# Quarter sums on DVE, LayerNorm's scale and shift on transposed tiles (ACT) and later on h (GpSimd), in a hybrid decoder layer on one core

## Chip, cores and metric

The kernel runs on 1 core of one Trainium2 chip. The metric is the device time of one launch in microseconds (us). The version before takes 1103.41 us, the median of three runs between 1101.94 and 1104.91. Engines are named as the profile names them: PE is the matrix engine (TensorE), DVE is VectorE, ACT is ScalarE, POOL is GpSimd, and SP is the engine that issues all the DMAs here.

## The reference

One decoder layer over 512 rows of 1024 numbers, in float32, in four steps that each end with a LayerNorm over `ALPHA*x + step(x)`:

```python
h = LN1(ALPHA*h + 0.5*swiglu(h, w_ffn1_in, w_ffn1_out))     # silu(gate)*up, 1024 -> 2816 -> 1024
h = LN2(ALPHA*h + mixer(h))     # HGRN2 heads (chunks of 64) and causal pooling, then w_mix_out
h = LN3(ALPHA*h + cross_attention(h, mem))                  # 4 heads, 256 memory tokens
h = LN4(ALPHA*h + 0.5*swiglu(h, w_ffn2_in, w_ffn2_out))
# LN(x, g, b) = (x - mean) * rsqrt(var + eps) * g + b, over the 1024 numbers of a row
```

## The kernel before

**Number format.** A float32 operand is split into two parts of a reduced matmul format: ACT casts the source (`hi`, line 65), DVE subtracts the cast from the source (`lo`, line 66), and PE sums three products, hi·hi, hi·lo and lo·hi (lines 54 to 56 in projections, 248 to 250 in `out_gemm`, 366 in the feed-forward). So each block of weights and each activation costs a cast, a subtraction and, for a weight, a DMA of 512 KB from SP.

**Feed-forward (`ffn`).** The 2816 hidden columns go in 22 blocks of 128 (the first two of ffn1 by plain products, "first"). Each other block multiplies a gate and an up weight as quarters, by seven products instead of eight: `a11`, `a12`, `s1`, `s4`, `s2`, `s3`, `a22`, each of 12 matmuls of 128x256 with a weight "quad" (128x512, a cast and a subtraction). Four sums per block, done on POOL (`sums`, lines 345 to 348), make the quarters s1 to s4 of the weight, in the buffers into which it was loaded. On the side of the activations the quarters `b11`, `b21`, `b22` are parts of the transposed input, and `t1` to `t4` are sums of them: for ffn1 sums of x on POOL (line 122), for ffn2 made while the third LayerNorm's tiles are transposed (`transpose_quarters`). Blocks go in pairs; one group of two blocks (two groups in ffn2) has its `a12` and `a11` started ahead. A pair is 168 matmuls.

**Output product and LayerNorm (`out_gemm`).** Each of the four steps ends here: two halves of 512 columns, and in each four accumulators for the four tiles t of 128 rows. In the second half the last four blocks of weights are kept, so that the tiles end one after the other, tile 0 first. At a tile's end DVE adds `alpha*h` (line 263), takes the statistics (266, 172, 174), POOL raises the variance to the power -1/2 (`rstd`, 176), and DVE applies everything in `ln_tile`: `(h - mean)*G`, then `*rstd + B`, each as two halves (lines 178 to 184), with G and B as rows broadcast to all partitions. Then PE transposes the tile by eight 128x128 matmuls against `ident` (line 191, into `trh`), and the transposed parts are split straight from PSUM into the tiles of the next step's input (`f1T` for the mixer, `moT` for attention, `xob`/`xot` for ffn2). The last step writes to the output instead.

**Mixer.** It projects with `wf`, `wq`, `wg`, `wi` and `wv`, then makes the scores within a chunk by levels m = 1 to 64 (`lv1` to `lv64`, line 553). Each level multiplies, in two halves, by QP and KR; behind each half DVE multiplies that half of QP and KR in place by decays (`Tlev`, lines 567 and 568) for the next level. POOL makes the decays (546) and, at four levels, the pooling windows (`pl`, 504 to 509).

**What sets the order.** A framework schedules the instructions at build time and writes one fixed list for each engine; on the chip each list is executed strictly in order, and an instruction that waits holds all behind it. Buffers come from pools: `raw` (7 of 128x1024, where every weight lands, and G and B too), `q` (7 split weights), `b8` (13 large ones), `sm` (small ones). A DMA into a buffer can start only when the last reader of what was there is done, and SP issues its DMAs in order too.

Of the kernel before, what the change touches and what calls it, by code (L numbers as in the profile page):

```python
# [23 lines left out]
H = 4  # L24
# [9 lines left out]
def layer_kernel(ctx: ExitStack, tc: tile.TileContext, a, out):  # L34
# [82 lines left out]
    xs = [b8([P, 2, 4, 256], F32, f"xs{i}") for i in range(2)]  # L117
    for n, t, x, y in (("t1", xs[0][:, 0], xf[0][:, :, lo_], xf[0][:, :, hi_]),
                       ("t2", xs[0][:, 1], xs[0][:, 0], xf[1][:, :, hi_]),
                       ("t3", xs[1][:, 0], xf[0][:, :, hi_], xf[1][:, :, hi_]),  # L120
                       ("t4", xs[1][:, 1], xs[0][:, 1], xf[1][:, :, lo_])):
        nc.gpsimd.tensor_tensor(out=t, in0=x, in1=y, op=ALU.add)
        T = quarter(f"x{n}")
        split(t, T[:, :, 0, :], T[:, :, 1, :])
        xq[n] = parts(T)
# [3 lines left out]
    masks = const.tile([P, len(LEVELS), 64], F32, name="masks")  # L129
    nc.sync.dma_start(masks, a["masks"])  # L130
    masks = masks.bitcast(I32)
    identu = ident.bitcast(I32)
    recip = const.tile([P, 16], F32, name="recip")
    nc.sync.dma_start(recip, a["recip"].partition_broadcast(P))
    mhalf = const.tile([P, 4], F32, name="mhalf")
    nc.vector.memset(mhalf, -0.5)
    hlb = const.tile([P, 2, H], F32, name="hlb")
    nc.sync.dma_start(hlb, a["hgrn_lb"])
    gn = const.tile([P, 1], F32, name="gn")
    nc.sync.dma_start(gn, a["gnorm"])  # L140
# [12 lines left out]
    nc.vector.tensor_tensor(out=lsum, in0=le[:, 0, :], in1=le[:, 1, :], op=ALU.add)
    nc.vector.reciprocal(lsum, lsum)
    lb = const.tile([P, H], F32, name="lb")
    nc.vector.tensor_tensor(out=lb, in0=le[:, 0, :], in1=lsum, op=ALU.mult)
    oml = const.tile([P, H], F32, name="oml")
    nc.vector.tensor_scalar(oml, lb, -1.0, 1.0, op0=ALU.mult, op1=ALU.add)

# [3 lines left out]
    def ln_bcast(g, b):  # L163
        G, B = raw4([P, D], "G"), raw4([P, D], "B")
        nc.sync.dma_start(G, g.partition_broadcast(P))
        nc.sync.dma_start(B, b.partition_broadcast(P))
        return G, B

    def ln_tile(t, stats, GB, eps):
        G, B = GB  # L170
# [5 lines left out]
        nc.gpsimd.tensor_tensor(out=rstd, in0=ve, in1=mhalf[:, 0:1], op=ALU.pow)  # L176
        for hf in range(2):
# [4 lines left out]
            nc.vector.scalar_tensor_tensor(  # L182
                out=h[t][:, sl], in0=h[t][:, sl], scalar=rstd, in1=B[:, sl],
                op0=ALU.mult, op1=ALU.add)

    def transpose_h(t, tiles):
        for hf in range(2):
            ps = tr_ps(f"trh{t}{hf}")
            for j in range(4):
                k = hf * 4 + j  # L190
                nc.tensor.transpose(ps[:, j * P:(j + 1) * P], h[t][:, k * P:(k + 1) * P], ident)
            pv = ps.rearrange("p (a b n) -> p a b n", a=2, b=2)
            for q in range(2):
                T = tiles[hf * 2 + q]
                tsl = slice(t * P, (t + 1) * P)
                split(pv[:, q], T[:, :, 0, tsl], T[:, :, 1, tsl])

    def transpose_quarters(t, q, f):
# [3 lines left out]
        pv = []  # L202
        for hf in range(2):
            ps = tr_ps(f"trh{t}{hf}")
            for j in range(4):
                k = hf * 4 + j
                nc.tensor.transpose(ps[:, j * P:(j + 1) * P], h[t][:, k * P:(k + 1) * P], ident)
            pv.append(ps.rearrange("p (k n) -> p k n", k=4))
# [3 lines left out]

        if t < 2:
            for hf in range(2):
                into(f"b{hf + 1}1", pv[hf])
                nc.scalar.copy(out=f["lo"][:, hf, :, usl], in_=pv[hf])
            return
        acc, low, b12 = f["lo"][:, 0, :, usl], f["lo"][:, 1, :, usl], f["b12"][:, :, usl]
        nc.vector.tensor_tensor(out=acc, in0=acc, in1=pv[0], op=ALU.add)
        into("t1", acc)  # L220
        nc.scalar.copy(out=b12, in_=pv[0])
        into("b22", pv[1])
        nc.vector.tensor_tensor(out=acc, in0=acc, in1=pv[1], op=ALU.add)
        into("t2", acc)
        nc.vector.tensor_tensor(out=b12, in0=b12, in1=pv[1], op=ALU.add)
        into("t3", b12)
        nc.vector.tensor_tensor(out=acc, in0=acc, in1=low, op=ALU.add)
# [601 lines left out]
```

## Time and profile before

| | |
|---|---|
| median of three runs | 1103.41 us (1101.94 to 1104.91) |
| the profiled execution, its own time | 1105.94 us |
| its span | 1104.1 us |
| PE busy | 1071.0 us, 97% (6782 instructions) |
| DVE busy | 779.4 us, 71% |
| ACT busy | 457.7 us, 41% |
| POOL busy | 324.0 us, 29% |
| transfers on SP's queue | 112.78 MB, mean 102 GB/s of HBM reads and writes over the span |

Read it so. The span is the time between the first and the last instruction of one profiled execution, some 2 us less than that execution's own time. An engine's busy time is the sum of its instructions; on PE a matmul counts as busy from its modelled start to its end. In the lists below, a row such as `a<-b 128x512 x4 | ...` names the tile that is written, those that are read, its shape and how often it comes. A part in brackets, `[4.39 <-PE f1ps L250]`, is the idle time ahead of the instruction on its engine, and what ended it. In the timeline the first number is the start in us from the span's beginning, the second the duration. In the windows view the first pair is the stretch.

The stages lie as follows: start of ffn1 14 to 46 us, its loop to about 242, its output product to about 360, mixer to 560, attention to 750, ffn2 from 750 on.

### The profile page before, as it was taken

Reading aid. Unit: us, or ns where it says so; the run is one execution under the profiler, and the core shown is the slowest. Engines: PE = TensorE matmul, PEld = TensorE weight load, DVE = VectorE, ACT = ScalarE, POOL = GpSimd, SP = SyncE. Lnnn points to the kernel's source line nnn. Section 1 sums busy time; section 2 is a strip of 40 time slices with the busy share of each in tenths; the row PEclk is TensorE's granted clock in tenths of the full one; section 3 lists DMA queues with packets and bytes.
Section 4 is the critical chain, followed back from the end, with each engine's and each line's share of the span. In section 5 each row is a group of like instructions: output and inputs, shape, how many; then the busy total and the mean of one; then the engine's idle time right before and its main releaser. Section 6 shows DMA issues by size and latency. Waiting matters only on the chain.

```text
span 1104.1 us, 17228 instructions
## 1 busy us (share of the span) xinstructions
PE 1071.0 (97%) x6782; PEld 970.4 (88%) x6782; DVE 779.4 (71%) x1160; ACT 457.7 (41%) x812; POOL 324.0 (29%) x226
## 2 busy tenths in 40 slices
PE   8799999999999999999999999977999999999997
PEld 7799999998888888889888988856999999988885
DVE  7899999984425633675786356488999999982416
ACT  6455555572211332224324345044555555572210
POOL 5666756700000020401010000017567576400001
PEclk9999999999999999999999999988999999999999
DMA  7324233263331322212427411111332432443402
GB/s 278 144 87 143 77 114 116 78 181 100 112 127 44 115 77 77 86 58 80 138 68 220 125 58 56 59 39 58 113 118 77 126 104 80 149 135 96 134 1 76
DMA packets 34495, 113.87 MB, mean 103 GB/s; under 512 B 4336, under 2 KB 5616, under 8 KB 34416
## 3 DMA queue, kind: packets, MB, share of 16 engines
q1 hardware_dynamic: 34416, 112.78, 31.9%
q8 instruction: 53, 0.87, 0.3%
q14 instruction: 26, 0.21, 0.1%
HBM read 110.67 MB, written 2.10 MB: 102 GB/s over the span
## 4 chain that ended last, share of the span: by engine, by line
PE 91%; DVE 3%; DMA 2%; POOL 1%; issue 1%; ACT 1%; SPq 0%; DVEq 0%; ACTq 0%; POOLq 0%
PE f2u L366 11%; PE f1u L366 10%; PE f2v L366 5%; PE f1v L366 5%; PE f1ps L248 4%; PE f1ps L249 4%; PE f1ps L250 4%; PE f2ps L250 4%; PE f2ps L248 4%; PE f2ps L249 4%; PE f2w L366 3%; PE f1w L366 2%; PE lv L553 2%; PE pxq L56 1%; PE pxq L54 1%; PE pxq L55 1%
## 5 line engine op out<-in xcount | busy, mean ns | idle before, releaser
L176 POOL TENSOR_TENSOR rstd<-ve,mhalf 128x1 f32<-128x1 f32 x16 | 15.5, 970 | 482.3 <-DVE ve L174 482.3
L66 DVE TENSOR_TENSOR wlo_f<-raw_f,whi_f 128x1024 fp32r<-128x1024 f32 x40 | 48.8, 1223 | 98.5 <-PE f1ps L249 46.4
L65 ACT CAST whi_f<-raw_f 128x1024 fp32r<-128x1024 f32 x40 | 42.1, 1052 | 113.4 <-PE f2ps L250 55.3
L366 PE MATMUL f2u<-xot,qf2s 128*128 128x256 f32 x528 | 68.4, 287 | 3.1 <-DVE f2sg L380 3.1
L366 PEld LDWEIGHTS f2u<-xot,qf2s 128*128 128x128 f32 x528 | 66.1, 195 | 3.6 <-DVE f2sg L380 3.6
L248 PE MATMUL f1ps<-whi_f,f1gs 128*128 128x512 f32 x160 | 62.5, 390 | 0.0
L249 PE MATMUL f1ps<-wlo_f,f1gs 128*128 128x512 f32 x160 | 62.3, 389 | 0.0
L249 PE MATMUL f2ps<-wlo_f,f2gs 128*128 128x512 f32 x160 | 62.3, 389 | 0.0
L248 PE MATMUL f2ps<-whi_f,f2gs 128*128 128x512 f32 x160 | 62.3, 389 | 0.0
L250 PE MATMUL f1ps<-whi_f,f1gs 128*128 128x512 f32 x160 | 62.1, 391 | 0.0
L250 PE MATMUL f2ps<-whi_f,f2gs 128*128 128x512 f32 x160 | 61.9, 390 | 0.0
L366 PE MATMUL f1u<-xt,qf1s 128*128 128x256 f32 x480 | 60.7, 283 | 0.0
L366 PEld LDWEIGHTS f1u<-xt,qf1s 128*128 128x128 f32 x480 | 59.0, 192 | 0.0
L66 DVE TENSOR_TENSOR qf2a<-raw_f2g,qf2a 128x512 fp32r<-128x512 f32 x44 | 53.2, 1214 | 7.9 <-ACT qf2a L65 6.7
L345 POOL TENSOR_TENSOR f2s<-raw_f2u 128x512 f32<-128x512 f32 x22 | 35.5, 1615 | 72.7 <-DMA raw_f2u<-in_w2in 69.9
L66 DVE TENSOR_TENSOR qf1a<-raw_f1g,qf1a 128x512 fp32r<-128x512 f32 x40 | 50.3, 1261 | 7.2 <-ACT qf1a L65 6.4
L366 PE MATMUL f2u<-xob,qf2a 128*128 128x256 f32 x264 | 39.0, 296 | 9.6 <-ACT qf2a L65 6.1
L345 POOL TENSOR_TENSOR f1s<-raw_f1u 128x512 f32<-128x512 f32 x20 | 31.2, 1561 | 57.9 <-DMA raw_f1u<-in_w1in 37.8
L366 PEld LDWEIGHTS f2u<-xob,qf2a 128*128 128x128 f32 x264 | 35.7, 203 | 11.2 <-ACT qf2a L65 7.0
L366 PE MATMUL f2w<-xob,qf2a 128*128 128x256 f32 x264 | 36.7, 290 | 2.0 <-DVE qf2a L66 0.8
L347 POOL TENSOR_TENSOR raw_f2g<-f2s,raw_f2g 128x512 f32<-128x512 f32 x22 | 36.7, 1669 | 0.9 <-DVE qf2a L66 0.6
L366 PEld LDWEIGHTS f2w<-xob,qf2a 128*128 128x128 f32 x264 | 34.1, 197 | 2.7 <-DVE qf2a L66 1.0
(325 smaller groups left out, 3135.8 us busy)
## 6 DMA issues: line engine op xcount, KB each, us to landing
raw_f<-in_w1out SPq DMA_DIRECT2D x22, 512.0 KB, 3.8
raw_f2g<-in_w2in SPq DMA_DIRECT2D x22, 512.0 KB, 3.7
raw_f2u<-in_w2in SPq DMA_DIRECT2D x22, 512.0 KB, 4.5
raw_f<-in_w2out SPq DMA_DIRECT2D x22, 512.0 KB, 3.7
raw_f1g<-in_w1in SPq DMA_DIRECT2D x20, 512.0 KB, 4.3
raw_f1u<-in_w1in SPq DMA_DIRECT2D x20, 512.0 KB, 4.5
raw_wk<-in_wk SPq DMA_DIRECT2D x8, 512.0 KB, 3.9
raw_mo<-in_wmixo SPq DMA_DIRECT2D x8, 512.0 KB, 3.6
```

What stands on the lines that cost most here:

```text
L54: nc.tensor.matmul(o, lh, rh, start=first, stop=False)
L55: nc.tensor.matmul(o, lh, rl, start=False, stop=False)
L65: nc.scalar.copy(out=hi, in_=src)
L66: nc.vector.tensor_tensor(out=lo, in0=src, in1=hi.bitcast(F32), op=ALU.subtract)
L176: nc.gpsimd.tensor_tensor(out=rstd, in0=ve, in1=mhalf[:, 0:1], op=ALU.pow)
L248: nc.tensor.matmul(ps[t], ah[:, tsl], wh, start=i == 0 and j == 0, stop=False)
L249: nc.tensor.matmul(ps[t], ah[:, tsl], wl, start=False, stop=False)
L250: nc.tensor.matmul(ps[t], al[:, tsl], wh, start=False, stop=i == nb - 1 and j == 1)
L345: nc.gpsimd.tensor_tensor(out=s1, in0=a21, in1=a22, op=ALU.subtract)
L347: nc.gpsimd.tensor_tensor(out=a11, in0=s1, in1=a11, op=ALU.subtract)
L366: nc.tensor.matmul(o, q[:, w, wsl], x[k][r], start=opens and k == 0 and n == 0, stop=ends and k == 3 and n == 2, skip_group_check=True)
L553: nc.tensor.matmul(ps[:, i * 64:(i + 1) * 64].rearrange("p (n m) -> p n m", m=m), KR[:, hd, cs], rhs, start=True, stop=True)
```

## The change

Nothing of what is computed changes, apart from rounding.

1. **Weight sums of the feed-forward** (`sums`) go from POOL to DVE.
2. **Sums of x** for ffn1 (`x_sums`) go from POOL to DVE, and stand behind the first two blocks' `a12` and `a11` instead of ahead of everything.
3. **LayerNorm 1 to 3.** `normalize` no longer applies G and B. DVE makes `nmr = -mean*rstd`, ACT applies `rstd*h + nmr` in two halves of 128x512, PE transposes, and ACT applies the scale and shift of each column while it moves the transposed parts to SBUF: after the transpose a column is a partition, so these are eight Identity activations of 128x128 a tile with one number per partition from a new constant `lnT`. The result `y` is then split.
4. **h itself** gets its scale and shift later (`restore`): eight operations of 128x1024 on POOL for each of the three LayerNorms, programmed at the head of the next `out_gemm`, with G and B loaded there. The final LayerNorm (`ln_final`) is as before.
5. **Quarters for ffn2** are added from the SBUF tiles y on DVE; t4 comes only after the last tile.
6. **Order of the blocks.** A block's `a12` and `a11` are begun by a rule (`begin(4)`: at most four blocks open) after s4 and s2 and after s3 of a pair; ffn1 opens with 2 blocks, ffn2 with 3 instead of 4. One more split weight block is kept in `b8` (`head + 3`).
7. **Constants of the mixer** (masks, recip, hlb and what is worked out from it) stand behind ffn1 in the program.

```diff
-        nc.gpsimd.tensor_tensor(out=t, in0=x, in1=y, op=ALU.add)
+    def x_sums():
+            nc.vector.tensor_tensor(out=t, in0=x, in1=y, op=ALU.add)
...
-    def ln_tile(t, stats, GB, eps):
+    def normalize(t, stats, eps):
+        mv, rstd = moments(stats, eps)
+        nc.vector.tensor_scalar(nmr, mv[:, 0:1], rstd, -1.0, op0=ALU.mult, op1=ALU.mult)
+        for hf in range(2):
+            sl = slice(hf * 512, hf * 512 + 512)
+            nc.scalar.activation(h[t][:, sl], h[t][:, sl], AF.Identity, scale=rstd, bias=nmr)
+    def restore(ln, g, b):
+        G, B = rows(g, "G"), rows(b, "B")
+        for t in range(NT):
+            nc.gpsimd.tensor_tensor(out=h[t], in0=h[t], in1=G, op=ALU.mult)
+            nc.gpsimd.tensor_tensor(out=h[t], in0=h[t], in1=B, op=ALU.add)
...
+    def transposed(t, hf, y, ln):
+            nc.tensor.transpose(ps[:, j * P:(j + 1) * P], h[t][:, k * P:(k + 1) * P], ident)
+            nc.scalar.activation(y[:, j, :], ps[:, j * P:(j + 1) * P], AF.Identity,
+                                 scale=lnT[:, ln, 0, k:k + 1], bias=lnT[:, ln, 1, k:k + 1])
...
-            ws = [wblock(wsrc[hf, order[i]], f"{name}{hf}_{i}", stay=hf == 1 and i < head + 2) for i in range(head, nb)]
-            if hf == 1:
-                GB = ln_bcast(g, b)
+            ws = [wblock(wsrc[hf, order[i]], f"{name}{hf}_{i}", stay=hf == 1 and i < head + 3) for i in range(head, nb)]
+            if hf == 1 and final:
+                GB = rows(g, "G"), rows(b, "B")
...
-            nc.gpsimd.tensor_tensor(out=s1, in0=a21, in1=a22, op=ALU.subtract)
+            nc.vector.tensor_tensor(out=s1, in0=a21, in1=a22, op=ALU.subtract)
...
+            begin(4)
+            for j in two:
+                product(j, "s3")
+            begin(4)
```

The change moves instructions; three places show it.

PE at the end of ffn1's output product, before. `f1ps` are the accumulators, `h_306` and `h_307` the tiles t = 2 and 3 of h, `trh` the transposes, and `pf` the mixer's first two projections, which read the transposed input `f1T` and the weights wf0 and wf1 (`whi_wf`, `wlo_wf`):

```order
L250 MATMUL f1ps_3290<-whi_f_10_3495,f1gs_3210 128x512
L191 MATMUL trh_3660<-ident,h_306 128x128 x4
L248 MATMUL f1ps_3290<-whi_f_10_3495,f1gs_3210 128x512
L249 MATMUL f1ps_3290<-wlo_f_10_3496,f1gs_3210 128x512
L250 MATMUL f1ps_3290<-whi_f_10_3495,f1gs_3210 128x512
L54 MATMUL pf_3739<-f1T_3539,whi_wf_3729 128x256
L55 MATMUL pf_3739<-f1T_3539,whi_wf_3729 128x256
L56 MATMUL pf_3739<-f1T_3539,wlo_wf_3730 128x256
...
L191 MATMUL trh_3705<-ident,h_307 128x128 x4
L191 MATMUL trh_3714<-ident,h_307 128x128 x4
```

The same place after, where `h_267` is tile 3:

```order
L267 MATMUL f1ps_3268<-wlo_f_10_3473,f1gs_3188 128x512
L268 MATMUL f1ps_3268<-whi_f_10_3472,f1gs_3188 128x512
L186 MATMUL trh_3706<-ident,h_267 128x128 x4
L186 MATMUL trh_3719<-ident,h_267 128x128 x4
L54 MATMUL pf_3772<-f1T_3512,whi_wf_3762 128x256
L55 MATMUL pf_3772<-f1T_3512,whi_wf_3762 128x256
L54 MATMUL pf_3773<-f1T_3512,whi_wf_3768 128x256
```

Before, 48 matmuls of pf (on the rows of tiles 0 and 1) stood between the last matmul of the output product and the transposes of tile 3; after, the transposes stand right behind it, and all of pf behind them. Between mixer and attention the same is so, with `pk` and `wk3` in place of pf and wf0.

ACT at that place, after. `y` is the transposed tile in SBUF with scale and shift:

```order
L159 ACTIVATE h_267<-h_267,nmr,rstd 128x512 x2
L189 ACTIVATE y_3705<-trh_3706,lnT 128x128 x4
L65 CAST f1T_3512<-y_3705 128x2x128
L65 CAST f1T_3513<-y_3705 128x2x128
L189 ACTIVATE y_3705<-trh_3719,lnT 128x128 x4
L65 CAST f1T_3514<-y_3705 128x2x128
L65 CAST f1T_3515<-y_3705 128x2x128
L65 CAST whi_wf_3762<-raw_wf_3760 128x1024
L65 CAST whi_wf_3768<-raw_wf_3766 128x1024
```

Before, ACT cast wf0 and wf1 ahead of all the casts of f1T; now both stand behind the last tile's.

POOL in the mixer's levels, before (`pl` are the pooling windows, `rs` the heads' root mean squares behind the levels):

```order
L509 TENSOR_TENSOR pl_4448<-pl_4447 128x512
L503 MEMSET pl_4534 128x16
L503 MEMSET pl_4535 128x16
L509 TENSOR_TENSOR pl_4534<-pl_4533 128x512
L640 TENSOR_TENSOR rs<-ss,mhalf 128x4 x4
```

And after:

```order
L558 TENSOR_TENSOR pl_4481<-pl_4480 128x512
L552 MEMSET pl_4567 128x16
L552 MEMSET pl_4568 128x16
L164 TENSOR_TENSOR h_264<-h_264,G 128x1024
...
L164 TENSOR_TENSOR h_267<-h_267,G 128x1024
L558 TENSOR_TENSOR pl_4567<-pl_4566 128x512
L165 TENSOR_TENSOR h_264<-h_264,B 128x1024
...
L165 TENSOR_TENSOR h_267<-h_267,B 128x1024
L689 TENSOR_TENSOR rs<-ss,mhalf 128x4 x4
```

The multiplications by G stand ahead of the last pooling window, the additions of B behind it. In all POOL's list falls from 215 to 68 rows and DVE's grows from 1011 to 1169; ACT's goes from 744 to 776, PE's from 3181 to 3183.

More of the change, by code (lines that the diff above doesn't have):

```diff
@@ L195, in transpose_h, with transpose_quarters @@
                 tsl = slice(t * P, (t + 1) * P)
[L196 to L198 removed]
+                yv = y[:, hf * 4 + q * 2:hf * 4 + q * 2 + 2, :]
+                split(yv, T[:, :, 0, tsl], T[:, :, 1, tsl])
+    def transpose_quarters(t, q, f, ln):
         u = t % 2
         usl = slice(u * P, (u + 1) * P)
[L202 to L208, printed above, removed]
@@ L222, in transpose_quarters @@
-        into("b22", pv[1])
-        nc.vector.tensor_tensor(out=acc, in0=acc, in1=pv[1], op=ALU.add)
+        y1 = half(1)
+        into("b22", y1)
+        add(acc, acc, y1)
         into("t2", acc)
-        nc.vector.tensor_tensor(out=b12, in0=b12, in1=pv[1], op=ALU.add)
-        into("t3", b12)
-        nc.vector.tensor_tensor(out=acc, in0=acc, in1=low, op=ALU.add)
-        into("t4", acc)
-    def out_gemm(wsrc, nkt, act, alpha, g, b, eps, name, final=False, order=None, stay=4, quarters=False):
+        add(y0, y0, y1)
@@ L232, in out_gemm @@
+        into("t3", y0)
+        if t == 3:
+            for u in range(2):
+                usl = slice(u * P, (u + 1) * P)
+                acc = f[u][:, :4, :]
+                add(acc, acc, f[u][:, 4:, :])
+                into("t4", acc)
+    def out_gemm(wsrc, nkt, act, alpha, g, b, eps, name, final=False, order=None, stay=4, quarters=False,
+                 ln=None, prev=None):
         nb = nkt // 2
         order = list(range(nb)) if order is None else order
-        tiles = f = None
+        tiles, f = None, {}
+        if prev is not None:
+            restore(*prev)
@@ L312, in layer_kernel, with ffn @@
     BANK = {"a11": "u", "s2": "u", "s3": "u", "a22": "u", "s1": "v", "s4": "v", "a12": "w"}
-    def ffn(win, wout, X, g, b, name, final, first=None, lead=1):
+    def ffn(win, wout, X, g, b, name, final, first=None, lead=2, ln=None, prev=None):
         gt = [b8([P, 4, S], F32, f"{name}g{q}") for q in range(-(-FT // 4))]
```

213 lines of the change are left out of this document (116 added, 97 removed).

## The prediction

> **What bounds the kernel now.** I read the windows by stage first. Columns: stretch, its length, then busy us (xcount) of PE, PEld, DVE, ACT and POOL, granted TensorE clock, DMA share, GB/s.
>
> ```profile
> 14.00:46.00 32.00, 23.61 (x132) 19.69 (x132) 30.12 (x30) 15.35 (x26) 24.62 (x13) 1.00 0.49 174
> 46.00:242.00 196.00, 196.00 (x1616) 195.61 (x1616) 181.01 (x236) 111.31 (x213) 113.35 (x76) 0.99 0.37 119
> 340.00:372.00 32.00, 31.53 (x180) 26.80 (x179) 24.92 (x49) 7.54 (x18) 3.96 (x4) 1.00 0.21 68
> 420.00:500.00 80.00, 80.00 (x460) 69.01 (x459) 50.49 (x172) 18.58 (x30) 14.41 (x16) 1.00 0.24 76
> 556.00:590.00 34.00, 33.97 (x221) 30.38 (x220) 30.64 (x58) 12.71 (x26) 3.94 (x4) 1.00 0.33 103
> 730.00:778.00 48.00, 33.16 (x205) 30.43 (x205) 41.68 (x55) 23.38 (x46) 25.31 (x17) 0.82 0.23 68
> 776.00:978.00 202.00, 201.94 (x1676) 201.61 (x1676) 184.75 (x243) 115.52 (x220) 117.98 (x72) 1.00 0.36 115
> ```
>
> PE is the bound nearly everywhere: both ffn loops (46:242, 776:978), ffn1's LayerNorm into the mixer (340:372), the mixer (420:500) and its LayerNorm into attention (556:590). It loses time in two places: 8.4 us idle at the start of ffn1 (14:46), and 14.8 us, at a clock of 0.82, where the third LayerNorm hands over to ffn2 (730:778). More can't come back. The waits of PE around the second place name quads that ACT and DVE had not split:
>
> ```profile
> PE f2u L366 <- ACT qf2a L65: 6.1, 3, 4.8
> PE f2u L366 <- DVE qf2a L66: 3.4, 1, 3.4
> ```
>
> An idle stretch costs twice. After 750:756, with PE busy 2.36 of 6 us, six us run at half clock; after 42:46, four run at 0.61:
>
> ```profile
> 42.00:46.00 4.00, 0.47 (x3) 0.27 (x3) 2.37 (x3) 3.02 (x7) 3.77 (x3) 0.96 0.00 0
> 46.00:50.00 4.00, 4.00 (x23) 4.00 (x24) 3.49 (x7) 1.91 (x5) 0.00 (x0) 0.61 0.59 184
> 750.00:756.00 6.00, 2.36 (x18) 1.95 (x16) 6.00 (x7) 2.03 (x4) 5.29 (x4) 0.97 0.29 87
> 756.00:762.00 6.00, 5.35 (x25) 5.35 (x26) 5.03 (x8) 2.13 (x5) 3.58 (x3) 0.50 0.00 0
> ```
>
> That is 4 x 0.39 = 1.6 and 6 x 0.50 = 3 us; I add 2 us to a long gap. The Trainium skill, "TensorE: Matmul & The Clock Gate" (Part 1: The HAM clock gate), has the clock halve after an idle window of some 3.4 us until one such busy window has passed, and calls the ramp too small to model; its half rate is the 0.50 of the row, its window would make 1.7 us of each gap instead of 2 (1 us less in the sum), and leaving the ramp out some 6 less.
>
> The timeline of DVE and POOL at the start (start, duration, operation) shows the second rule of this kernel:
>
> ```profile
> 14.46 0.68 DVE L66 TENSOR_TENSOR xT<-xf,xT 128x512 fp32r<-128x512 f32 x1
> 15.06 2.89 DVE L66 TENSOR_TENSOR qx<-rawx,qx 128x512 fp32r<-128x512 f32 x1
> 17.37 2.84 POOL L122 TENSOR_TENSOR xs<-xf,xf 128x1024 f32<-128x1024 f32 x1
> 17.88 2.88 DVE L66 TENSOR_TENSOR xT<-xf,xT 128x512 fp32r<-128x512 f32 x1
> ...
> 389.28 2.13 POOL L546 TENSOR_TENSOR Tlev<-T 128x1024 f32<-128x1024 f32 x1 [20.74 <-DVE T L453]
> ```
>
> A DVE operation with two operands in SBUF takes 0.68 us alone and 2.9 beside a POOL operation: they take turns, and DVE sits out a whole POOL operation, which alone lasts 2.13.
>
> **The change, part by part.**
>
> *Start of ffn1: -5.5.* POOL has nothing left there, so four splits of 2.9 us become 0.68 (about 9 us off DVE); the sums of x come back as four DVE operations behind the first products. PE's "first" ends some 3 us earlier, and the s4 quad for which it stands in 42:46 comes some 5 earlier, behind the x sums on DVE. Bounds -2 (only "first") and -8.4 (all idle).
>
> *ffn loops: +4.*
>
> ```profile
> 203.36 1.29 DVE L66 TENSOR_TENSOR qf1s<-raw_f1g,qf1s 128x512 fp32r<-128x512 f32 x2
> 204.56 0.42 DVE L373 TENSOR_TENSOR f1sg<-f1sg,f1u 128x256 f32<-128x256 f32 x1
> 204.90 1.29 DVE L66 TENSOR_TENSOR qf1s<-raw_f1g,qf1s 128x512 fp32r<-128x512 f32 x2
> raw_f1u<-in_w1in SPq DMA_DIRECT2D x20, 512.0 KB, 4.5
> ```
>
> Alone, a split or sum costs DVE 0.60 (two in 1.20 until the next start), an evacuation 0.34. A pair of blocks has 14 splits, now 8 sums, and 12 evacuations: 13.2 + 4.1 = 17.3 us, against 168 matmuls at 196.00/1616 = 0.12, 20.2 us of PE. It fits, but DVE is in order: each pair's first sum stands in its queue ahead of splits, waits for the u block that the a22 split before it set free (4.5 us), two operations later the next u block is issued (4.5), and 10.7 us of work close the circle: 4.5 + 1.2 + 4.5 + 10.7 = 20.9. Before, that wait was POOL's. With 4.1 for each transfer it is 20.1. I take 20.5: 0.3 us for 17 pairs, less what the seven quad buffers let DVE lead at first. Bounds 0 and +12. No other cost: the two extra table loads and the mixing constants meet an ACT busy 111 of 196 us.
>
> *LayerNorm into the mixer and into attention: +27.*
>
> ```profile
> 343.98 0.69 DVE L263 SCALAR_TENSOR_TENSOR h<-h,f1ps 128x512 f32<-128x512 f32 x1 [4.39 <-PE f1ps L250]
> 344.71 0.69 DVE L266 BATCH_NORM_STATS2 stats<-h 128x6 f32<-128x512 f32 x1
> 345.44 0.21 DVE L172 BATCH_NORM_AGGREGATE mv<-stats 128x2 f32<-128x12 f32 x1
> 345.92 0.99 POOL L176 TENSOR_TENSOR rstd<-ve,mhalf 128x1 f32<-128x1 f32 x1 [116.36 <-DVE ve L174]
> 347.07 1.41 DVE L182 SCALAR_TENSOR_TENSOR h<-h,rstd,B 128x512 f32<-128x512 f32 x2
> 347.88 1.32 PE L191 MATMUL trh<-ident,h 128*128 128x128 f32 x8
> 349.43 0.65 ACT L65 CAST f1T<-trh 128x256 fp32r<-128x256 f32 x2 [0.49 <-DVE f1T L66]
> 513.07 0.28 ACT L637 ACTIVATE o<-o 128x128 f32<-128x128 f32 x1
> 513.33 0.28 ACT L637 ACTIVATE o<-o 128x128 f32<-128x128 f32 x1
> 17.44 1.05 ACT L65 CAST xt<-xs 128x1024 fp32r<-128x1024 f32 x1 [0.83 <-POOL xs L122]
> L66 DVE TENSOR_TENSOR wlo_f<-raw_f,whi_f 128x1024 fp32r<-128x1024 f32 x40 | 48.8, 1223 | 98.5 <-PE f1ps L249 46.4
> ```
>
> The four scale-and-shift operations (2.8 us a tile) go, but rstd lay beside them and is now in the open: from a tile's last matmul 0.73 + 0.73 + 0.24 + 0.24 + 0.99 to rstd, 0.25 for nmr, 0.6 for the first Identity (half the 128x1024 cast, and its fixed part): 3.9 us as before, 4.5 where two lo splits of the tile before stand between. PE now has the transposes after 14 to 17 matmuls of the next tile, 3.2 to 3.9 us: some 0.8 lost for each of three tiles, 2.4.
>
> For the last tile the cover itself is moved. Before, 48 matmuls of pf, and of pk after the mixer, lay between its last matmul and its transposes; now the transposes stand right behind it, and ACT casts wf0 (wk3) only behind all of that tile's work. So PE waits 4.5 for h, 0.6 for four transposes, on ACT twice 4 x 0.25 + 0.65 = 3.3, the weight's cast 1.05 and its lo split 1.22: 10.7 us, in which it has 1.3 of its own. 9.4 idle, 2.4 at the tiles, 2 of clock: 13.8 at each, less the 0.5 idle in 340:372. Bounds: 5 each (h alone) to 15.
>
> *h*G + B in the mixer: +12.*
>
> ```profile
> 463.89 1.22 DVE L66 TENSOR_TENSOR wlo_wg<-raw_wg,whi_wg 128x1024 fp32r<-128x1024 f32 x1
> G<-in_ln_g SPq DMA_DIRECT2D x4, 512.0 KB, 4.3
> 472.47 0.68 DVE L568 TENSOR_TENSOR KR<-KR,Tlev 128x512 f32<-128x512 f32 x1
> 473.74 2.45 PE L553 MATMUL lv<-QP,KR 128*128 128x64 f32 x21
> 473.75 1.44 POOL L509 TENSOR_TENSOR pl<-pl 128x512 f32<-128x512 f32 x1 [5.66 <-ACT pl L504]
> 480.54 0.69 DVE L568 TENSOR_TENSOR KR<-KR,Tlev 128x512 f32<-128x512 f32 x1
> 483.63 2.56 PE L553 MATMUL lv<-QP,KR 128*128 128x64 f32 x22
> ```
>
> G is issued where the wg1 split frees a buffer (465.1) and lands at 469.5. Four POOL multiplications take turns with the decays L567 and L568, which have both operands in SBUF: by 2.13 + 0.6 each they end near 480, and the last decay of lv8 at 480.6 instead of 473.15. PE needs it for the second half of lv16 at 475.6: 5.0 lost. pool_in(0) (473.75) is queued behind them. B waits for G's buffer, and SP holds mraw4 to mraw7 and the mo blocks behind it, which are needed later; it lands at 484.6, and its four additions delay the decays of lv16 from 481.2 to 495.6. By the same steps PE loses 1.4 and 3.7 at lv32, 0.5 at lv64. Together 10.5, and 1.5 of clock. Bounds 0 (DVE always first) and 13.
>
> *The same for attention: +0.5* (0 to 4); POOL is free there and DVE not half busy. *For ffn2's output: +9.* G comes after the s2 split of block 19, B after it. Eight POOL operations of 2.13 lock DVE out for 17 us. From there DVE has 17.3 us of work in one pair and some 10 in the last ten splits, PE 20.2 + 14.4: 7.3 us to spare, 9.7 short. Bounds 0 and 13. The w2out blocks queue on SP behind B, land some five us before PE wants them, and cost nothing.
>
> *LayerNorm into ffn2: -9.* In 730:778 PE did 16 products of 12 matmuls (1.44 us), 23 us, in 47.6: 24.5 lost. With the new order: transposes of tile 3 behind three a11 products, and h3's nmr queued on DVE behind tile 2's sums and splits, 4.4 us; s1 of block 0 waits 1.6 for t1; the quads of blocks 0 and 1 come from DVE at 0.6 each, 4.6; the tiles 1.5; clock 3: 15. Bounds -3 and -15. The block more in b8 and lead=3 are in this order and cost nothing of their own; the final LayerNorm is as it was.
>
> **Sum.** -5.5 + 4 + 27 + 12 + 0.5 + 9 - 9 = +38 on the profiled execution's 1105.94 (span 1104.1 and 1.8 around it), 1144; on the median of 1103.41, 2.5 less, 1141.
>
> **Rivals.** *POOL's share is hidden*, chance 0.2: the two-input DVE operations get in first and the multiplications fill their gaps; without the 21.5 us of h*G + B it gives 1120. For it: DVE is busy only 50 of 80 us in 420:500. Against it: the 2.9 us rows. The Trainium skill, "GPSIMD Engine Reference" (4.1 Engine selection), puts element-wise work on VectorE and GPSIMD at half its rate: by that alone the sums moved the right way, h*G + B the wrong way but off the path, and the time is this rival's.
>
> *The LayerNorm chains are covered*, chance 0.12: nothing slower. Place: the tile ends of all three hand-overs. If h is ready within some 3 us of a tile's last matmul and ACT's weight casts follow at once, the 27 go and the hand-over to ffn2 gains 11 more: 38 - 27 - 11 = 0, 1103, and under it if the start gains more. For it: ACT is idle most of 340:372. Against it: rstd alone is there after 2.9 us, and ACT's queue is in order.
>
> *The u transfers set the loops*, chance 0.1: at 20.9 a pair, +12 instead of +4: 1149.
>
> **Chances.** The forecast has 0.58, 1127 to 1156 with its bounds. The range reaches down under the first rival, 1114 to 1156. About 0.3% (3 us) can be told from no change: slower by more 0.86, within it 0.05, faster 0.09, both from the second rival and a little of the others.
>
> **What would show it.** PE idle some 9 us at each of the two LayerNorms, with wf0's and wk3's cast as ACT's last step before PE goes on; L164 and L165 near 2.1 to 2.7 us, DVE operations of 2.7 beside them, and lv16 and lv32 waiting for KR; ffn pairs of 20.2 to 20.9 with DVE waiting for raw_f1u; 730:778 with some 12 us idle. It is wrong if PE stays over 97% busy, if the casts of wf0 and wk3 come early, or if DVE passes POOL at 0.68.

## The result, and the profile after

The changed kernel takes 1137.39 us, the median of four runs between 1137.25 and 1138.30; before takes 1104.16 us, the median of four runs (1101.94 to 1105.17). The ratio is 1.031, with a 95% interval from 1.029 to 1.032: slower by 33 us, and some 4 us under the forecast of 1141. The profiled execution lasted 1137.40 us, its span 1135.5. Of nine later timings of the kernel before, one took 2953.74 us; it is left out of the ratios given below.

Where it went is read from the starts of PE's tiles, as the timelines of both kernels show them. Each row is the stretch from the first matmul of one tile to the first of the next; before sums to 1104.1, after to 1135.5.

| stretch (first tile to next) | before us | after us | difference | forecast |
|---|---|---|---|---|
| start and ffn1's loop, to `f1ps` | 240.28 | 233.55 | -6.7 | -5.5 + 2 |
| ffn1's output product, into the mixer, to `pq` | 147.21 | 160.58 | +13.4 | +13.8 |
| rest of the projections, to `lv` | 47.47 | 47.46 | 0 | 0 |
| the levels, to `krt` | 72.23 | 83.50 | +11.3 | +12 |
| states, to `mops` | 20.02 | 20.02 | 0 | 0 |
| mixer's output product, into attention, to `vm` | 63.05 | 77.13 | +14.1 | +13.8 |
| attention, to `xops` | 90.43 | 90.45 | 0 | +0.5 |
| attention's output product and ffn2's loop, to `f2ps` | 295.65 | 295.30 | -0.4 | -9 + 2 + 9 |
| ffn2's output product and the end | 127.76 | 127.51 | -0.3 | 0 |

The windows of the changed kernel, by the same columns as those of before:

```profile
34.00:46.00 12.00, 9.91 (x63) 9.10 (x63) 10.63 (x16) 8.76 (x16) 0.00 (x0) 0.86 0.27 89
46.00:233.00 187.00, 187.00 (x1558) 186.74 (x1557) 159.20 (x303) 107.27 (x206) 0.53 (x6) 1.00 0.35 112
340.00:369.00 29.00, 18.85 (x92) 14.14 (x90) 11.25 (x31) 23.39 (x58) 1.65 (x3) 0.91 0.17 55
480.00:500.00 20.00, 15.48 (x76) 13.00 (x74) 20.00 (x36) 4.17 (x10) 17.60 (x8) 0.83 0.19 60
595.00:622.00 27.00, 18.05 (x126) 17.33 (x127) 14.14 (x24) 16.63 (x32) 0.54 (x1) 0.81 0.52 159
762.00:780.00 18.00, 13.04 (x78) 12.22 (x78) 17.62 (x32) 14.21 (x32) 0.93 (x1) 0.72 0.00 1
960.00:1008.00 48.00, 40.63 (x305) 39.96 (x304) 43.58 (x52) 21.14 (x38) 21.66 (x8) 0.89 0.40 135
```

The loop of ffn1 is full, as before, with DVE busy 159 of 187 us instead of 181 of 196. PE has new holes in four places: 340:369 (into the mixer), 480:500 (the levels), 595:622 (into attention) and 960:1008 (the last pairs of ffn2). In the third column from the right, the granted clock, these four windows have 0.81 to 0.91 of full speed. PE's waits name what came late:

```profile
PE trh L186 <- ACT h L159: 17.6, 12, 4.6
PE f2u L382 <- DVE f2sg L396: 6.9, 2, 6.3
PE lv L602 <- DVE KR L617: 5.9, 3, 3.5
PE pk L54 <- ACT whi_wk L65: 4.4, 2, 4.3
PE pf L54 <- ACT whi_wf L65: 4.0, 1, 4.0
```

The twelve waits for h are those of the twelve tiles of the first three LayerNorms; three of them are the last tile's, 4.0 to 4.6 us each. Then come the weight casts of wk and wf, the decays of the levels, and one long wait at ffn2's end.

### The profile page after: what moved, and what is told of

It reads as the page before. It is cut to its first block, busy times and chain, and to the rows that moved or that the text cites. A ratio compares the mean times of both kernels' runs of the same rounds, so it can differ in the third digit from the quotient of the medians.

```text
span 1135.5 us, 17175 instructions
## 1 busy us (share of the span) xinstructions
PE 1083.4 (95%) x6782; PEld 980.1 (86%) x6782; DVE 745.3 (66%) x1296; ACT 506.3 (45%) x928; POOL 102.1 (9%) x78
## 4 chain that ended last, share of the span: by engine, by line
PE 83%; DVE 9%; ACT 3%; issue 3%; DMA 1%; POOL 1%; DVEq 0%; POOLq 0%; ACTq 0%
PE f1u L382 10%; PE f2u L382 8%; PE f1v L382 5%; PE f2v L382 4%; PE f2ps L268 4%; PE f2ps L266 4%; PE f2ps L267 4%; PE f1ps L268 3%; PE f1ps L267 3%; PE f1ps L266 3%; PE f2w L382 2%; PE f1w L382 2%; DMA raw_f2u<-in_w2in 1%; PE lv L602 1%; PE pxq L54 1%
## 5 line engine op out<-in xcount | busy, mean ns | idle before, releaser
L65 ACT CAST whi_f<-raw_f 128x1024 fp32r<-128x1024 f32 x38 | 40.0, 1052 | 102.8 <-PE f2ps L268 46.7
L266 PE MATMUL f1ps<-whi_f,f1gs 128*128 128x512 f32 x152 | 59.2, 390 | 0.0
L266 PE MATMUL f2ps<-whi_f,f2gs 128*128 128x512 f32 x152 | 59.2, 389 | 0.0
L268 PE MATMUL f1ps<-whi_f,f1gs 128*128 128x512 f32 x152 | 58.8, 390 | 0.0
L268 PE MATMUL f2ps<-whi_f,f2gs 128*128 128x512 f32 x152 | 58.8, 390 | 0.0
L159 ACT ACTIVATE h<-h,nmr,rstd 128x512 f32<-128x512 f32 x24 | 18.2, 806 | 83.5 <-DVE nmr L156 83.5
L164 POOL TENSOR_TENSOR h<-h,G 128x1024 f32<-128x1024 f32 x12 | 32.2, 2710 | 251.7 <-DMA G<-in_ln_g 251.7
L150 POOL TENSOR_TENSOR rstd<-ve,mhalf 128x1 f32<-128x1 f32 x16 | 11.3, 706 | 422.2 <-DVE ve L148 422.2
L189 ACT ACTIVATE y<-trh,lnT 128x128 f32<-128x128 f32 x96 | 36.2, 468 | 1.5 <-PE trh L186 1.0
L382 PE MATMUL f2u<-xob,qf2a 128*128 128x256 f32 x264 | 35.4, 283 | 0.0
L602 PEld LDWEIGHTS lv<-QP,KR 128*128 128x128 f32 x224 | 27.8, 202 | 8.7 <-DVE KR L617 7.1
L382 PE MATMUL f2v<-xob,qf2s 128*128 128x256 f32 x264 | 34.0, 284 | 0.8 <-DVE qf2s L66 0.5
L382 PE MATMUL f1v<-xT,qf1s 128*128 128x256 f32 x240 | 32.4, 292 | 2.1 <-ACT qf1s L65 2.1
```

Source lines behind the costliest of these rows:

```text
L65: nc.scalar.copy(out=hi, in_=src)
L159: nc.scalar.activation(h[t][:, sl], h[t][:, sl], AF.Identity, scale=rstd, bias=nmr)
L164: nc.gpsimd.tensor_tensor(out=h[t], in0=h[t], in1=G, op=ALU.mult)
L189: nc.scalar.activation(y[:, j, :], ps[:, j * P:(j + 1) * P], AF.Identity, scale=lnT[:, ln, 0, k:k + 1], bias=lnT[:, ln, 1, k:k + 1])
L266: nc.tensor.matmul(ps[t], ah[:, tsl], wh, start=i == 0 and j == 0, stop=False)
L268: nc.tensor.matmul(ps[t], al[:, tsl], wh, start=False, stop=i == nb - 1 and j == 1)
```

## The experiments

All times are compared with the changed kernel's 1137.4 us; kernels timed once stand beside it, where its four runs lay within 1.1 us. Stages are cut as in the table above. A stage can differ between two executions of one kernel: `f1ps` begins between 232.5 and 234.1 us in the kernels that share the changed kernel's start.

**Weights of the next projection split ahead of the tiles (`early`).**

```diff
+            if hf == 1 and early is not None:
+                early()
...
+    def early_f():
+        for hd in range(2):
+            W["f", hd] = wblock(a["wmix"][4 + hd], f"wf{hd}")
+
+    def early_k():
+        for k in (3, 4):
+            W["k", k] = wblock(a["wk"][k], f"wk{k}")
...
-    pf01 = proj_T2([wblock(a["wmix"][FF_ + hd], f"wf{hd}") for hd in range(2)], X1, "pf")
+    pf01 = proj_T2([W["f", hd] for hd in range(2)], X1, "pf")
```

> The changed kernel (1137.4 us) with the weights of the first two projections of the mixer (wf0, wf1) and the first two memory keys of attention (wk3, wk4) loaded and split ahead of the tiles of the output product, so that PE has some 40 of their matmuls behind its last one and ahead of tile 3's transposes, as before the change. LayerNorm is as in the changed kernel. Theory (the lost cover and the weight cast at the end of ACT's queue cost 10.5 us at each place): some 9 to 11 us less at each, 1115 to 1120. Rival (the longer chain over ACT is the cost, whatever stands beside it): PE runs out of cover and waits for f1T instead, under 4 us less at each, 1130 to 1137.

Measured: 1120.42 us, 17.0 less, at the upper end of the theory. Into the mixer the stage is 149.3 us long, 11.3 less and 2 above before. PE's timeline at that place (start, duration, operation, idle time ahead and what ended it; rows between are pf's other matmuls):

```profile
358.70 0.39 PE L268 MATMUL f1ps<-whi_f,f1gs 128*128 128x512 f32 x1
358.93 0.28 PE L54 MATMUL pf<-f1T,whi_wf 128*128 128x256 f32 x1
...
363.73 0.66 PE L186 MATMUL trh<-ident,h 128*128 128x128 f32 x4 [0.56 <-ACT h L159]
```

pf starts behind the last `f1ps` at once, its matmuls last until h of tile 3 is ready 5 us later, and PE idles 0.56 us. LayerNorm is the same, with all its operations on ACT. So all but some 2 us of the cost into the mixer was the missing cover (matmuls for PE while it waits, and the weights' casts that they need, which go together). Into attention the gain is only 6.0 (71.1 us): two keys are 48 matmuls of 0.12, 5.8 us, and behind them the third key's weight is cast after tile 3's work again, `PE pk L54 <- ACT whi_wk L65: 3.6, 2, 3.3` in that kernel's waits. The kernel `best1` below splits four keys ahead; there the stage is 65.8 us, 2.7 above before.

**h*G + B on POOL at other places (`moved`).**

```diff
-        if prev is not None:
-            restore(*prev)
...
+                if hf == 0 and prev is not None and i == (3 if final else 0):
+                    restore(*prev)
...
+    restore(0, a["ln1_g"], a["ln1_b"])
```

> The changed kernel with h*G + B moved on POOL to where DVE has few operations with two SBUF operands: for the mixer's output behind the projection of q, for ffn2's output behind the third weight block of its output product; attention's stays. Theory (the turns between POOL and DVE at the decays of lv16 to lv64 and at the last pair of ffn2 cost 11 us each): 1137.4 - 22 = 1115, up to 1120 if G and B hold buffers that wi needs. Rival (the levels and the last pair lose their time to something else of the change, the sums on DVE among them): 1134 to 1138. A second rival (the cost moves along with the operations): over 1130, with decays and splits of 2.7 us at the new places.

Measured: 1130.52 us, 6.9 less: by the total the second rival, by stage the theory in the mixer and the second rival in ffn2. The levels are 72.24 us long, as before the change: the 11.3 are gone. But the block loads run far ahead, so in ffn2 G landed at the loop's end, not in the output product, and the cost went along: loop 4.8 shorter, output product and end 7.6 longer. The waits of PE there, and DVE's first activation splits for the output product:

```profile
PE f2ps L266 <- DVE f2gs L66: 3.7, 1, 3.7
PE f2u L382 <- DVE f2c L399: 2.7, 1, 2.7
```

```profile
996.97 9.75 DVE L66 TENSOR_TENSOR f2gs<-f2g,f2gs 128x1024 fp32r<-128x1024 f32 x5
```

Five splits in 9.75 us, 1.95 each. The place chosen was wrong; the mechanism stands, since the cost followed the operations.

**h*G + B on DVE (`restdve`).** One word in each of the two lines:

```diff
-            nc.gpsimd.tensor_tensor(out=h[t], in0=h[t], in1=G, op=ALU.mult)
+            nc.vector.tensor_tensor(out=h[t], in0=h[t], in1=G, op=ALU.mult)
```

> The changed kernel with h*G + B on DVE instead of POOL at all three places, and nothing else; in the new order it stands behind the last level in the mixer, among the projections of q in attention, and in ffn2's output product. Theory (what cost 11 us each was DVE sitting out POOL's operations; the work itself is 9.8 us of DVE where it has room): 1137.4 - 22 = 1115, up to 1120. Rival (DVE's own 9.8 us delay the splits and the output product instead): 1122 to 1137.

Measured: 1117.59 us, 19.8 less, as the theory says. The groups of DVE in this kernel and of POOL in the changed one:

```profile
L164 DVE TENSOR_TENSOR h<-h,G x12: 1211/1215/1226, 507.1 to 978.9; 128x1024 f32<-128x1024 f32 x12
```

```profile
L164 POOL TENSOR_TENSOR h<-h,G 128x1024 f32<-128x1024 f32 x12 | 32.2, 2710 | 251.7 <-DMA G<-in_ln_g 251.7
```

1.22 us on DVE (the middle of the three figures is the median in ns) against 2.71 on POOL, during which DVE operations with both operands in SBUF waited (rows of 2.8 us below). In the mixer the scheduler puts DVE's operations behind the levels (507 to 525 us), so engine and place changed together there. In ffn2 they ran at the loop's end (960 to 982), not in the output product, as was expected: at the place where POOL had them, among the same splits, they cost PE a wait of 2.8 us instead of 7.4. There the engine made the difference.

**Weight sums back on POOL (`sumspool`).**

```diff
-            nc.vector.tensor_tensor(out=s1, in0=a21, in1=a22, op=ALU.subtract)
+            nc.gpsimd.tensor_tensor(out=s1, in0=a21, in1=a22, op=ALU.subtract)
...
```

> The changed kernel with the four weight sums per block back on POOL. Theory (the loops are bound by PE with the sums on either engine; what the sums on DVE bring is the hand-over to ffn2 and the start, where DVE no longer sits out POOL's sums): loops at 20.2 us a pair, 6 to 12 us more at the hand-over and the start together, 1143 to 1150. Rival (the hand-over gained from the new LayerNorm and from the lead of three blocks alone): 1135 to 1139.

Measured: 1148.41 us, 11.0 more. ffn1 ends its loop at 233.6 as in the changed kernel: there the sums cost PE nothing on either engine. All of it is in the stage from `xops` to `f2ps`, 306.0 against 295.3. With the sums on POOL PE is busy this much in the hand-over (first two rows), and in the changed kernel (rows of the second fence):

```profile
762.00:785.00 23.00, 14.60 (x87) 13.10 (x86) 20.51 (x26) 14.94 (x33) 12.45 (x10) 0.70 0.00 1
785.00:810.00 25.00, 20.58 (x153) 19.80 (x152) 17.28 (x29) 14.73 (x30) 12.81 (x8) 0.93 0.37 116
```

```profile
762.00:785.00 23.00, 17.19 (x106) 15.76 (x105) 21.04 (x39) 18.76 (x42) 0.93 (x1) 0.78 0.08 24
785.00:810.00 25.00, 24.99 (x206) 24.83 (x207) 24.07 (x46) 16.39 (x32) 0.00 (x0) 1.00 0.43 148
```

240 matmuls have a record in the one and 312 in the other. 72 at 0.12 are 8.6 us, of which 0.6 is a later start: 8 of the 10.7 us. Of the rest 1.7 shows at the last pairs, where POOL now has sums and h*G + B (PE waits 9.1 us there, instead of 7.4).

**Sums of x back on POOL (`xspool`).**

```diff
-            nc.vector.tensor_tensor(out=t, in0=x, in1=y, op=ALU.add)
+            nc.gpsimd.tensor_tensor(out=t, in0=x, in1=y, op=ALU.add)
```

> The changed kernel with the four sums of x on POOL again, but at their new place behind the first products. Theory (the start gained because DVE no longer takes turns with POOL): DVE splits of 2.9 us beside them, 3 to 6 us lost again, 1140 to 1143. Rival (the later place alone brought it): 1136 to 1139.

Measured: 1140.12 us, 2.7 more, and `f1ps` begins 3.2 us later: the low end of the theory. The scheduler put the sums between 9 and 23 us, ahead of the first products a12 and a11 again, so place and engine went back together. So of the 6.7 us gained at the start some 3.2 are the sums of x; the other 3.5 are not separated (the mixing constants' DMAs and DVE operations, which no longer stand in the start, are a candidate that wasn't tried).

**One more weight buffer (`raw8`).**

```diff
-        return wp.tile(shape, F32, tag="raw", name=name, bufs=7)
+        return wp.tile(shape, F32, tag="raw", name=name, bufs=8)
```

> The changed kernel with eight weight buffers instead of seven. In it each pair's first sum waits on DVE for its u block, and DVE's pairs are 20.9 us apart against PE's 20.2. Theory (that circle over the buffers eats DVE's lead, and h*G + B meets a DVE without lead): with one buffer more the waits for u blocks shrink, and the 7.4 us of PE's wait at the last pairs fall to 0 to 4: 1129 to 1134. Rival (DVE's lead is held down by the seven split buffers, or POOL's turns cost 11 us at any lead): 1136 to 1138.

Measured: 1136.96 us, by the total the rival. By stage it is not: DVE's waits for the u blocks (the up weight's, `raw_f2u`) fall from 18.4 us to 4.4 in ffn2, its pairs stand 20.1 us apart instead of 20.5 to 20.9, and the stage to `f2ps` is 291.7, 3.6 less. But the mixer's G also found a buffer earlier and landed at 466.9 instead of 475.8, POOL met the decays one level sooner, and from `lv` to `o` it took 2.7 us longer. Two effects of one edit cancelled; the lead of DVE does soften POOL's turns, by some third.

**The old LayerNorm at the first two places (`oldln12`).** `ln_dve` is the old `(h - mean)*G`, `*rstd + B` on DVE, `transpose_old` the old transposes with splits from PSUM; both `prev` of ln1 and ln2 go.

```diff
-                    normalize(t, stats[t], eps)
                     if quarters:
+                        normalize(t, stats[t], eps)
+                    else:
+                        ln_dve(t, stats[t], GB, eps)
+                    if quarters:
...
-                        transpose_h(t, tiles, ln)
+                        transpose_old(t, tiles)
```

> The changed kernel with the LayerNorm of before at the first two places (scale and shift by DVE ahead of the transposes, splits straight from PSUM, no h*G + B later); the third LayerNorm and all else as changed. Theory (the new LayerNorm costs 13.4 us into the mixer, 14.1 into attention and 11.3 in the mixer's levels; the rest of the change gains as in the changed kernel): 1137.4 - 38.8 = 1098.6, within 1096 to 1102, faster than before. Rival (the sums on DVE or the mixing constants' new place share in those losses): 1106 or more.

Measured: 1097.17 us, 40.2 less. The stages into the mixer and into attention are 146.6 and 63.2 us long, as before the change, and the levels are back. So the first two LayerNorms with their h*G + B are the whole loss and more.

**The same, and ffn2's h*G + B on DVE (`best2`, again as `best2r`).** `restore_v` is `restore` with DVE operations, put inside the output product.

```diff
+                if hf == 0 and final and i == 6:
+                    restore_v(*prev)
```

> The kernel with the old first two LayerNorms, and ffn2's h*G + B done by DVE in the first half of its output product. Theory: 1098.6 - 11 = 1087.6, within 1085 to 1092. Rival (the last pair of ffn2 loses its time because DVE's lead over PE is used up by then, whatever POOL does): 1096 to 1100.

> The fastest kernel so far again (first two LayerNorms as before, the third as changed, ffn2's h*G + B by DVE in its output product, sums on DVE), timed in rounds against the kernel before. Expected: 1086 us, a ratio of 0.982 to 0.986 to before.

Measured: 1086.16 us, and timed again 1089.19 us (median of five, 1086.16 to 1092.1) against 1104.31 for before: a ratio of 0.986 (0.983 to 0.988), at the upper edge of what was expected of it. This kernel and `lead4` below, which can't be told apart, are the fastest found here. The stage to `f2ps` falls from 294.6 to 284.2, and to 286.1 in the second profile: the turns with POOL at ffn2's last pairs had cost 8.4 to 10.4. PE's waits at these pairs fall from 7.5 us to 0.9.

**The changed LayerNorm, mended (`best1`).** Kernel `early` with wk3 to wk5 ahead and wk6 ahead of tile 3's end, eight split buffers (not tried alone), the mixer's h*G + B behind the projection of q on POOL, and ffn2's on DVE as in `best2`.

> The changed kernel with its LayerNorm, and three mends: wf0, wf1, wk3, wk4, wk5 are split ahead of the tiles and wk6 ahead of tile 3's end (eight split-weight buffers instead of seven); the mixer's h*G + B stands behind the projection of q; ffn2's is done by DVE, eight operations of about 1.2 us in the first half of its output product. Theory (each cost was a missing cover or a turn with POOL, none the arithmetic itself): 1137.4 - 11.3 (wf) - 11 (wk) - 11.3 (levels) - 11 (last pair of ffn2) = 1093, within 1090 to 1098. Rival (the work added to DVE and ACT shows up again where it is put): 1100 or more, with PE waiting for weight splits in ffn2's output product.

Measured: 1092.46 us. PE's waits for wk, wf and the levels are gone:

```profile
PE trh L192 <- ACT h L159: 9.3, 12, 4.0
PE f1v L394 <- ACT qf1s L65: 2.1, 1, 2.1
...
PE f2u L394 <- DVE f2sg L408: 0.8, 1, 0.8
```

The same arithmetic on the same engines, apart from ffn2's h*G + B, takes 45 us less. Into attention the stage is 65.8 us instead of 77.1.

**All LayerNorms as before (`oldln3`).** `oldln12` with the third LayerNorm and `transpose_quarters` of before, and no h*G + B left.

```diff
-                        transpose_quarters(t, tiles, f, ln)
+                        transpose_quarters(t, tiles, f)
```

> All LayerNorms as before the change, the third with its transposes split straight from PSUM and its sums in t1 to t4 by DVE from PSUM; of the change there remain the sums on DVE, the sums of x, the order of the blocks and the mixing constants. No h*G + B later. Theory (the hand-over to ffn2 gained 11 us because DVE no longer sits out POOL's sums, and the new LayerNorm adds little): 1084 to 1090, level with the kernel that keeps the new third LayerNorm. Rival (the new third LayerNorm brought half of it or more): 1092 to 1098.

Measured: 1092.64 us, in the rival's range, at its low end; the ratio to before is 0.989 (0.988 to 0.991). The stage to `f2ps` is 290.2 us against 295.7 before, and 284.2 and 286.1 in the two profiles that keep the new third LayerNorm. So the theory was wrong: what is left of the change in this stage (the sums on DVE and the new order of the blocks, which are not separated here) brings 5.5 us, and the new LayerNorm another 4 to 6. Its largest wait is the one of before, for the quads that ACT and DVE had no time for:

```profile
PE f2u L396 <- ACT qf2a L65: 6.1, 3, 4.8
```

**Four blocks ahead (`lead4`).** `best2` with

```diff
-    ffn(a["w2in"], a["w2out"], X3, a["ln4_g"], a["ln4_b"], "f2", True, lead=3,
+    ffn(a["w2in"], a["w2out"], X3, a["ln4_g"], a["ln4_b"], "f2", True, lead=4,
```

> The fastest kernel with four blocks begun ahead in ffn2 instead of three. Theory (PE waits 4 us for tile 3 of the third LayerNorm because its ready products have run out, then runs at half clock): two more products of 1.44 us in that gap, 3 to 5 us less, 1081 to 1083. Rival (the fourth block's quads come from DVE later than tile 3, since DVE is busy all through the hand-over): 1085 to 1089.

Measured: 1087.89 us, 0.985 (0.984 to 0.987) of before, where `best2` has 0.986: as the rival said. The wait for tile 3 did go, and others came for it:

```profile
PE f2w L417 <- ACT y L219: 2.3, 1, 2.3
PE trh L216 <- ACT h L159: 2.2, 5, 0.6
...
PE f2w L417 <- DVE qf2a L66: 1.8, 1, 1.8
PE f2u L417 <- ACT whi_f L65: 1.2, 1, 1.2
```

By these waits the hand-over is bound by what DVE and ACT must do in it.

## Why the prediction was right, and where it was off

**LayerNorm into the mixer and attention: forecast 13.8 at each, measured 13.4 and 14.1.** PE after its last `f1ps`, then ACT, then DVE and POOL at the same place in the changed kernel:

```profile
358.26 0.40 PE L268 MATMUL f1ps<-whi_f,f1gs 128*128 128x512 f32 x1
363.29 1.82 PE L186 MATMUL trh<-ident,h 128*128 128x128 f32 x8 [4.63 <-ACT h L159]
369.13 0.58 PE L54 MATMUL pf<-f1T,whi_wf 128*128 128x256 f32 x1 [4.02 <-ACT whi_wf L65]
```

```profile
362.42 1.52 ACT L159 ACTIVATE h<-h,nmr,rstd 128x512 f32<-128x512 f32 x2 [1.71 <-DVE nmr L156]
364.02 1.50 ACT L189 ACTIVATE y<-trh,lnT 128x128 f32<-128x128 f32 x4
365.41 0.72 ACT L65 CAST f1T<-y 128x256 fp32r<-128x256 f32 x2
366.01 1.53 ACT L189 ACTIVATE y<-trh,lnT 128x128 f32<-128x128 f32 x4
367.39 0.74 ACT L65 CAST f1T<-y 128x256 fp32r<-128x256 f32 x2
367.99 3.92 ACT L65 CAST whi_wf<-raw_wf 128x1024 fp32r<-128x1024 f32 x4
```

```profile
361.59 0.55 POOL L150 TENSOR_TENSOR rstd<-ve,mhalf 128x1 f32<-128x1 f32 x1 [6.83 <-DVE ve L148]
```

From the last matmul to pf it is 10.5 us, where the sum had 10.7. That is nearer than its terms: h came after 4.6 (4.5 forecast), ACT's two rounds took 4.0 (3.3: the Identities of 128x128 follow each other at 0.35, not 0.25), and the weight's lo split of 1.22 cost nothing, since PE began with the products of the hi part. POOL's power took 0.55 us, not 0.99. The clock term of 2 us was 2.5: for five us behind the hole PE ran at half the clock.

```profile
369.00:374.00 5.00, 4.72 (x20) 4.40 (x21) 3.50 (x3) 4.20 (x5) 0.00 (x0) 0.50 0.74 230
374.00:394.00 20.00, 20.00 (x126) 18.15 (x126) 6.34 (x9) 4.62 (x6) 0.00 (x0) 1.00 0.29 101
```

That the cover, and not the longer chain, was the main reason is shown into the mixer by `early`, and into attention by `best1`: with it the stages are 2.1 and 2.7 us above before.

**h*G + B in the mixer: forecast +12, measured +11.3**, and `moved` shows that it comes from these operations at that place. With the 6.6 us by which the levels began later, G was to land at 476.1, and landed at 475.7; the last decay of lv8 was to end at 487.2, and ended at 487.0. POOL, the decays on DVE and PE's two halves of lv16:

```profile
475.77 10.69 POOL L164 TENSOR_TENSOR h<-h,G 128x1024 f32<-128x1024 f32 x4 [1.07 <-DMA G<-in_ln_g]
```

```profile
478.63 2.86 DVE L617 TENSOR_TENSOR KR<-KR,Tlev 128x512 f32<-128x512 f32 x1
482.46 1.79 DVE L616 TENSOR_TENSOR QP<-QP,Tlev 128x512 f32<-128x512 f32 x1
484.18 2.82 DVE L617 TENSOR_TENSOR KR<-KR,Tlev 128x512 f32<-128x512 f32 x1
```

```profile
481.55 2.00 PE L602 MATMUL lv<-QP,KR 128*128 128x64 f32 x16 [1.01 <-DVE KR L617]
487.06 3.68 PE L602 MATMUL lv<-QP,KR 128*128 128x64 f32 x16 [3.51 <-DVE KR L617]
```

Lv16 lost 4.5 us (5.0 forecast), but lv32 only 1.4 (5.1) and lv64 nothing: 5.9 of idle, not 10.5. The other 5 us are clock, not 1.5: 480:500 ran at 0.83 of full speed (3.4 us) and 500:526 at 0.93 (1.8). PE at half speed came later to lv32, so the slow clock took the place of the wait. The clock term was mis-sized, and the two errors cancelled.

**h*G + B in ffn2: forecast +9, measured +8.4 to +10.4** (`oldln12` against the two profiles of `best2`; the working had come to 9.7 and the sum took 9). POOL began at 970.39, DVE's splits took 2.8, and PE waited 6.3 us at 979.65:

```profile
970.39 11.01 POOL L164 TENSOR_TENSOR h<-h,G 128x1024 f32<-128x1024 f32 x4 [202.71 <-DMA G<-in_ln_g]
```

```profile
976.35 2.82 DVE L66 TENSOR_TENSOR qf2a<-raw_f2g,qf2a 128x512 fp32r<-128x512 f32 x1
979.10 0.41 DVE L396 TENSOR_TENSOR f2sg<-f2sg,f2u 128x256 f32<-128x256 f32 x1
979.43 2.52 DVE L66 TENSOR_TENSOR qf2a<-raw_f2g,qf2a 128x512 fp32r<-128x512 f32 x1
```

The row between the two splits is the rule in one line: the sum with an operand in PSUM takes 0.41 us as ever, its neighbours with both in SBUF wait for POOL. The Trainium skill, "SBUF — State Buffer" (Who interferes with whom), states it so: a DVE instruction with two SBUF inputs contends with a GpSimd instruction that reads SBUF, by an exclusive lock, and one with at most one, outside the 2-port perf modes, does not. These rows agree: 0.41 us between 2.82 and 2.52. The rival that hid POOL's share (1120) fell with them.

**The loops: forecast +4, measured about 0.** This is the step that failed. Its period came true: the first sums of two pairs in ffn2, waiting for their u block, are 20.9 us apart, as worked out (the last five pairs 20.5 to 20.9).

```profile
942.19 0.69 DVE L361 TENSOR_TENSOR f2s<-raw_f2u 128x512 f32<-128x512 f32 x1 [1.99 <-DMA raw_f2u<-in_w2in]
963.08 0.69 DVE L361 TENSOR_TENSOR f2s<-raw_f2u 128x512 f32<-128x512 f32 x1 [2.49 <-DMA raw_f2u<-in_w2in]
```

But PE never felt it, with 187.00 of 187 us busy in ffn1. DVE begins a loop by running ahead; the first sums of ffn1's third, fourth and fifth pair:

```profile
61.01 0.68 DVE L361 TENSOR_TENSOR f1s<-raw_f1u 128x512 f32<-128x512 f32 x1
...
77.89 0.69 DVE L361 TENSOR_TENSOR f1s<-raw_f1u 128x512 f32<-128x512 f32 x1 [1.43 <-DMA raw_f1u<-in_w1in]
...
97.09 0.69 DVE L361 TENSOR_TENSOR f1s<-raw_f1u 128x512 f32<-128x512 f32 x1 [0.53 <-DMA raw_f1u<-in_w1in]
```

The second begins at 47.14, so they stand 13.9, 16.9 and 19.2 us apart, and later ones 20.0 to 21.5, 20.6 in the mean. Against PE's 20.2 DVE gains some 10 us in those pairs and then gives back about 0.4 a pair. The sum had charged 17 pairs at 0.3, and put the lead down as a small deduction: the lead was the term that it had too small, since it is larger than what all later pairs take from it. `raw8` shows what is left of the circle: the 3.6 us at ffn2's end, where POOL's turns meet it. With it fell the rival that had the u transfers set the loops (1149).

**LayerNorm into ffn2: forecast -9, measured -8.8 to -10.8** (the stage's -0.4 less the 8.4 to 10.4). `oldln3` and `sumspool` divide it only in part: 5.5 from the sums on DVE with the new order of the blocks, 4 to 6 more with the new LayerNorm; with the new LayerNorm kept, sums on POOL cost 10.7. Wait for h3: 4.0 us, 4.4 forecast.

**Start: forecast -5.5, measured -6.7** to `f1ps`, 6.4 of it up to the first product s1; `xspool` gives back 3.2 to `f1ps`, 1.4 of it up to that product. Attention's h*G + B: 0.5 forecast, 0 measured.

**In sum** +31.4 of span against +38 forecast: the 4 of the loops, some 1.2 at the start, 0.7 in the levels, 0.5 in attention and some 0.6 in ffn2 and its end came out better, 0.5 at the two LayerNorms worse. The rival of covered LayerNorm chains (1103) fell at 340:369, where h came 4.6 us after the last matmul and ACT cast wf0 last. The pages of the profile split the loss another way: PE is idle for 52.1 us (1135.5 less 1083.4 busy) where it was 33.1 before, 19.0 more, and busy 12.4 us longer (1083.4 against 1071.0) with the same 6782 matmuls. The lower granted clock, 0.974 against 0.989, fits that, so some two fifths of the loss are matmuls that ran slower, and the rest is waiting.

## What to carry to other kernels

An arithmetic that moves off the path is only worth what the new order leaves on it: read, at every hand-over, what PE has to do between its last matmul and the first that needs the new data, and where the next weights' casts stand in an in-order queue. Splitting two weights earlier was worth 11 us at one place, with no operation changed. Work given to POOL is not free because POOL is idle: look at which DVE operations with two SBUF operands lie beside it, since here they took 1.8 to 2.9 us instead of 0.7. And an engine whose period is a little longer than PE's costs nothing while its lead lasts: count the lead at the start of a loop against the pairs.

## What the runs showed of the hardware that was not expected

The slow clock behind holes could be worth almost as much as their idle time: at the levels 5.9 us idle (the largest hole 3.5) and 5 us of clock. Into the mixer it was less, with 8.65 us idle (4.63 and 4.02) and 2.5 of clock. Over the span the mean granted clock was 0.974 against 0.989 before and 0.993 in `best1` and `best2`.

POOL's power of 128x1 took 0.55 us at the first ten tiles of the changed kernel, 0.93 at the last two of the third LayerNorm and 0.99 at the final one, where before all sixteen took 0.97 in the mean; no run tells why.

ACT's Identities of 128x128 from PSUM with one scale and bias per partition followed each other at 0.35 us, where those of the row of before that the sum used (a Square with a running sum) followed at 0.26.
